# ConvGLU by block products: seven for eight, up-projection and down-projection in two phases

## The chip, the cores and the metric

The program runs on one core of a Trainium2 chip. TensorE (PE) multiplies, VectorE (DVE), ScalarE (ACT) and GpSimd (POOL) work on SBUF tiles of 128 partitions, DVE and ACT read PSUM as well, and SyncE (SP) issues most DMA transfers. Each engine works through its own queue in a fixed order. The metric is the device time of one execution in microseconds (us).

## The reference

Two transformer layers over 1024 tokens of width 1024; layer 0 carries 256 context tokens too. In each layer attention is followed by this tail (`FF` is 2816):

```python
def _conv_ffn(h, w_up, conv_w, conv_b, w_down):
    gate, val = jnp.split(h @ w_up, 2, axis=-1)          # each [tokens, 2816]
    gate = conv over 3 neighbouring tokens, per feature, + conv_b
    return (jax.nn.silu(gate) * val) @ w_down

x = _layer_norm(ALPHA * x + g1 * y, ln1)                 # y: attention @ w_out
h = x * (1 + sc2) + sh2
x = _layer_norm(ALPHA * x + g2 * _conv_ffn(h, ...), ln2)
```

## The kernel before, in words

Every product is made in float32r as three passes: both operands are split into a high and a low part (`split_hi` L408 on POOL or L404 on ACT, `split_lo` L412 on DVE or POOL), and `three` multiplies high by high, high by low and low by high. Activations lie feature-major: features on partitions, tokens on the free axis, in chunks of 512 tokens (two; in layer 0 a third of 256 context tokens).

`layer_tail(l)` projects the attention's output, applies LN1 (`ln1`, with L1321 making the scaled rows and L1343 the residual, kept in SBUF as `acc`), then runs the ConvGLU over 22 tiles `f` of 128 features, and LN2 in `after`. For each tile the loop calls `up(f, 0)`, the gate's product (48 matmuls for each chunk of 512 tokens: 8 blocks of 128 input features, 3 passes, 2 chunks), then `down(f - 1)`, then `conv(f)`, then `up(f, 1)`, the value's product, then `glu(f)`. `down(f - 1)` multiplies the finished tile with its 128 rows of `w_down`: 8 output tiles by 2 chunks by 3 passes, 48 matmuls, each triple into a PSUM bank of its own that DVE adds to `acc` (L1400). `conv` is an ACT pass (L1367), two DVE passes (L1369, L1373) and Silu on ACT (L1377); `glu` is a DVE product (L1381) and the split of the result (ACT L404, DVE L412). The last two tiles are multiplied together after the loop by `last_down`. In layer 0 DVE also works at column sums of the next layer's `w_ada` (L552, eight instructions in each of the first 16 tiles).

The order of each engine's queue is set when the program is built: a scheduler places the recorded operations, engine by engine, from the order of the code and the pools' buffers. Weights are split by POOL ahead of their use.

## Time and profile before

| | us |
|---|---|
| median of 3 runs | 3625.1 (3624.45 to 3625.25) |
| the profiled execution: its span, which is its own time as far as it is recorded | 3624.5 |
| layer 0: ConvGLU tiles | about 1010 to 1867 |
| layer 1: ConvGLU tiles | about 2874 to 3566 |
| busy PE / DVE / ACT / POOL | 3444.8 / 2252.0 / 1281.6 / 1668.7 |

The rows quoted further down give one instruction's mean duration (in ns), or a stretch of time in us. A matmul's busy time is longer than its pace, since matmuls overlap: the pace is read from a run of them in the chain of waits, not from the mean. "Idle before" is how long an engine stood still in front of the instructions of a group, and the name behind the arrow is what ended it; such idle time costs nothing by itself when PE is busy beside it.

### The profile page before, as it was taken

Reading aid. Unit: us, or ns where it says so; the run is one execution under the profiler, and the core shown is the slowest. Engines: PE = TensorE matmul, PEld = TensorE weight load, DVE = VectorE, ACT = ScalarE, POOL = GpSimd, SP = SyncE. Lnnn points to the kernel's source line nnn. Section 1 sums busy time; section 2 is a strip of 40 time slices with the busy share of each in tenths; the row PEclk is TensorE's granted clock in tenths of the full one; section 3 lists DMA queues with packets and bytes.
Section 4 is the critical chain, followed back from the end, with each engine's and each line's share of the span. In section 5 each row is a group of like instructions: output and inputs, shape, how many; then the busy total and the mean of one; then the engine's idle time right before and its main releaser. Section 6 shows DMA issues by size and latency. Waiting matters only on the chain.

```text
span 3624.5 us, 50952 instructions
## 1 busy us (share of the span) xinstructions
PE 3444.8 (95%) x19450; PEld 2949.6 (81%) x19450; DVE 2252.0 (62%) x3434; ACT 1281.6 (35%) x2393; POOL 1668.7 (46%) x1804
## 2 busy tenths in 40 slices
PE   7998899979899999999998999999999999999997
PEld 5987787877788888888886787999997788888885
DVE  6687787873666666655455544777774555445555
ACT  4222777762411111111025334777773301111002
POOL 4532787643422222232223523888886533333333
PEclk9999999999999999999999999999999999999998
DMA  6367411664333322211104267233323211111111
GB/s 211 111 203 217 108 46 48 166 181 139 117 108 96 93 88 82 82 53 41 36 19 125 82 242 231 57 79 76 80 66 114 85 47 47 53 47 47 53 35 47
DMA packets 311952, 349.52 MB, mean 96 GB/s; under 512 B 19157, under 2 KB 233597, under 8 KB 311709
## 3 DMA queue, kind: packets, MB, share of 16 engines
q1 hardware_dynamic: 298508, 319.66, 30.4%
q10 hardware_dynamic: 11424, 18.94, 1.4%
q0 software_dynamic: 1776, 7.67, 0.6%
q8 instruction: 153, 2.51, 0.3%
q14 instruction: 91, 0.74, 0.1%
HBM read 275.04 MB, written 71.11 MB: 96 GB/s over the span
## 4 chain that ended last, share of the span: by engine, by line
PE 74%; POOL 8%; DVE 8%; issue 5%; DMA 4%; ACT 2%; SPq 0%; ACTq 0%; POOLq 0%; DVEq 0%
PE pu L417 29%; PE pd L417 15%; PE psum L194 7%; PE psum L335 5%; PE pso L417 4%; PE psum L304 4%; POOL p L264 3%; PE psq L417 2%; PE ps_f L417 2%; PE ps_tu L417 1%; DVE aa L552 1%; PE pw L417 1%; POOL pl L312 1%; DMA bias<-in_l_rpb_dram 1%; POOL st L261 1%
## 5 line engine op out<-in xcount | busy, mean ns | idle before, releaser
L1400 DVE SCALAR_TENSOR_TENSOR acc<-pd,mods,acc 128x512 f32<-128x512 f32 (+1 forms) x800 | 525.0, 697 | 267.0 <-PE pd L417 252.3
L408 POOL TENSOR_SCALAR fh_u<-fr_u 128x1024 fp32r<-128x1024 f32 x88 | 95.0, 1079 | 857.6 <-PE pu L417 479.9
L417 PE MATMUL pd<-ah,fh_d 128*128 128x512 f32 (+1 forms) x880 | 331.7, 377 | 6.3 <-DVE acc L1400 3.8
L417 PE MATMUL pd<-al,fh_d 128*128 128x512 f32 (+1 forms) x880 | 326.0, 370 | 0.5 <-DVE al L412 0.5
L417 PE MATMUL pd<-ah,fl_d 128*128 128x512 f32 (+1 forms) x880 | 325.9, 370 | 0.0
L194 PE MATMUL psum<-k,q 96*128 96x512 f32 (+1 forms) x1152 | 272.3, 373 | 6.7 <-DMA k<-kr_scr 4.0
L417 PE MATMUL pu<-h_1l,fh_u 128*128 128x512 f32 x704 | 275.1, 391 | 2.1 <-POOL h_1l L412 2.1
L417 PE MATMUL pu<-h_0h,fh_u 128*128 128x512 f32 x704 | 275.3, 391 | 0.0
L417 PE MATMUL pu<-h_0h,fl_u 128*128 128x512 f32 x704 | 275.0, 391 | 0.0
L417 PE MATMUL pu<-h_0l,fh_u 128*128 128x512 f32 x704 | 274.9, 391 | 0.0
L417 PE MATMUL pu<-h_1h,fh_u 128*128 128x512 f32 x704 | 274.3, 390 | 0.0
L417 PE MATMUL pu<-h_1h,fl_u 128*128 128x512 f32 x704 | 274.0, 389 | 0.0
L1381 DVE TENSOR_TENSOR cv<-cv,pu 128x1280 f32<-128x1280 f32 (+1 forms) x44 | 59.6, 1355 | 295.7 <-PE pu L417 289.1
L194 PEld LDWEIGHTS psum<-k,q 96*128 96x128 f32 x1152 | 196.4, 192 | 35.3 <-issue 4.4
L412 POOL TENSOR_TENSOR fl_u<-fr_u,fh_u 128x1024 fp32r<-128x1024 f32 x88 | 212.4, 2413 | 7.3
L552 DVE SCALAR_TENSOR_TENSOR aa<-aw,silu_late,aa 128x512 f32<-128x512 f32 x224 | 190.5, 880 | 37.1 <-DMA aw<-in_l_w_ada_dram 34.9
L417 PEld LDWEIGHTS pd<-ah,fh_d 128*128 128x128 f32 x880 | 166.1, 189 | 58.2 <-DVE acc L1400 5.1
L1377 ACT ACTIVATE cv<-cv 128x1280 f32<-128x1280 f32 (+1 forms) x44 | 51.4, 1169 | 443.0 <-DVE cv L1373 443.0
L264 POOL TENSOR_SCALAR p_m<-p_m,st_m 128x640 f32<-128x640 f32 x256 | 201.8, 801 | 12.6
L1367 ACT ACTIVATE cv<-pu,vec 128x1280 f32<-128x1280 f32 (+1 forms) x44 | 58.2, 1322 | 417.5 <-PE pu L417 417.5
L320 DVE TENSOR_TENSOR pl_m<-psum,ph_m 128x512 fp32r<-128x512 f32 x256 | 175.0, 684 | 37.7 <-ACT ph_m L314 36.7
L304 PE MATMUL psum<-ident,p_m 128*128 128x128 f32 x1280 | 192.9, 273 | 2.5 <-DVE pl_m L320 2.2
(499 smaller groups left out, 9817.1 us busy)
## 6 DMA issues: line engine op xcount, KB each, us to landing
aw<-in_l_w_ada_dram SPq DMA_DIRECT2D x96, 512.0 KB
fr_u<-in_l_w_up_dram SPq DMA_DIRECT2D x88, 512.0 KB
fr_d<-in_l_w_down_dram SPq DMA_DIRECT2D x44, 512.0 KB
fr_o<-in_l_w_out_dram SPq DMA_DIRECT2D x30, 512.0 KB
v<-v_scr SPq DMA_DIRECT2D x17, 640.0 KB
k_b<-k_scr SPq DMA_DIRECT2D x16, 640.0 KB
v_scr<-vev SPq DMA_DIRECT2D x40, 256.0 KB
k<-k_scr SPq DMA_DIRECT2D x15, 640.0 KB
```

Source lines behind the costliest of these rows:

```text
L194: nc.tensor.matmul(u["s"][bank][:, c:e], q[:, qc], ks, start=pi == 0, stop=pi == len(u["passes"]) - 1)
L264: nc.gpsimd.tensor_scalar(pt, pt, st[:, j, 7:8], 0.0, op0=ALU.mult, op1=ALU.add)
L304: nc.tensor.transpose(tp[:, off + bi * P : off + bi * P + P], pts[j][:, c : c + P], ident)
L320: nc.vector.tensor_tensor(pl[:, :w], tps[g][:, :w], ph[:, :w].bitcast(F32), ALU.subtract)
L335: nc.tensor.matmul(u["av"][:, q0 : q0 + bw], u["v"][:, kt, :], m[:, off : off + bw], start=first and part == 0, stop=last and part == 1, s ...
L408: nc.gpsimd.tensor_scalar(dst, src, 1.0, 0.0, op0=ALU.mult, op1=ALU.add)
L412: e.tensor_tensor(dst, src, hi.bitcast(F32), ALU.subtract)
L417: nc.tensor.matmul(ps, s, m, start=i == 0, stop=i == n - 1)
L552: nc.vector.scalar_tensor_tensor(accs[c], w, sck, accs[c], op0=ALU.mult, op1=ALU.add)
L1367: nc.scalar.activation(cv, g[:, :nt], AF.Identity, bias=vec(l, "cb", f), scale=vec(l, "w1", f))
L1381: nc.vector.tensor_tensor(cv, cv, v[:, :nt], ALU.mult)
L1400: nc.vector.scalar_tensor_tensor(acc[m][ci], ps[:, :cn], mod(l, ci // 2, 5, m), acc[m][ci], op0=ALU.mult, op1=ALU.add)
```

## The change

Gate and value are now one product of a 2 by 2 block matrix: rows are the two halves of the 1024 input features, columns are gate and value (weights A11, A12 for the gate, A21, A22 for the value, with 512 input features each), and the other operand's blocks are the halves of features by the two chunks of tokens. Seven block products replace eight. Each is 12 matmuls of 512 columns, so a tile takes 84 for 96. The weights' four sums (`weight_sums`: L1201, L1204, L1207, L1211) are made for every tile, the tokens' four sums (`token_sums`) once per layer in `ln1(1)`; every operand is split as before, the weights now by ACT (high) and POOL (low; the first product's by DVE in layer 1, the value's first half by DVE in layer 0). The context's chunk in layer 0 is still multiplied plainly.

The loop over tiles no longer calls `down`. After every second tile `keep_pair` makes the four sums of the activated pair and stores seven operands in DRAM (`a_scr`); the context's activations go to `ac_scr`, the last two tiles' to `al_scr`, and the residual of LN1 goes to `res_scr`. After the loop the pools are closed, and a second phase runs over the pairs, two at a time (five groups): for each of the seven products it splits weights and stored operands and makes 4 row tiles of 6 matmuls for each pair. P2, P3 and P4 are added to `acc` at once, the others collect in SBUF tiles `Q` and are added at the end. The last two tiles are multiplied plainly as before.

```diff
-        def up(f, part, order):
-            wh, wl = load_w(
-                cols(A[f"l{l}_w_up"][:, part * FF + f * P : part * FF + (f + 1) * P]), f"u{l}_{f}_{part}"
-            )
...
+    def weight_sums(A11, A12, A21, A22, tmp, eng):
+        e = [nc.vector if x == "dve" else nc.gpsimd for x in eng]
+        S1, S2 = tmp("s1"), tmp("s2")
+        e[0].tensor_tensor(S1, A21, A22, ALU.add)
+        yield "A21", A21
+        yield "P1", A11
+        e[1].tensor_tensor(S2, S1, A11, ALU.subtract)
+        yield "P6", S2
+        yield "P5", S1
+        e[2].tensor_tensor(A21, A11, A21, ALU.subtract)
+        yield "P7", A21
+        yield "P2", A12
+        yield "P4", A22
+        e[3].tensor_tensor(S2, A12, S2, ALU.subtract)
+        yield "P3", S2
+    def token_sums(B11, B12, B21, B22, tmp, eng):
+        e = [nc.vector if x == "dve" else nc.gpsimd for x in eng]
+        T1, T2, T3, T4 = (tmp(f"t{i}") for i in range(1, 5))
+        e[0].tensor_tensor(T1, B12, B11, ALU.subtract)
+        e[1].tensor_tensor(T2, B22, T1, ALU.subtract)
+        e[2].tensor_tensor(T3, B22, B12, ALU.subtract)
+        e[3].tensor_tensor(T4, B21, T2, ALU.subtract)
+        return {"P5": T1, "P6": T2, "P7": T3, "P4": T4}
...
+                xs = tl("ax", (512,), f"rs{l}_{ci}_{m}")[:, :cn]
+                nc.scalar.activation(xs, pb, AF.Identity, bias=der[:, 1, m : m + 1], scale=der[:, 0, m : m + 1])
+                nc.sync.dma_start(res_scr[l][m * P : (m + 1) * P, c0 : c0 + cn], xs)
...
+                for m, h in rows:
+                    whole[8 + m] = h
+                    if m < 4:
+                        continue
+                    parts(operand["P3"], m - 4, h, "dve")
+                    q = whole.pop(m - 4), whole.pop(m + 4), whole.pop(m), whole.pop(m + 8)
+                    sums = token_sums(
+                        *q, lambda n: tl("b", (512,), f"h{l}_{n}_{m}"), ("dve", "dve", "pool", "dve")
+                    )
+                    for i, p in enumerate(("P6", "P5", "P7", "P4")):
+                        parts(operand[p], m - 4, sums[p], "pool" if i % 2 else "dve")
...
+            b = [ps1(f"pu{l}_{f}_{i}") for i in range(3)]
+            bank = {"P1": b[0], "P2": b[0], "P6": b[1], "P7": b[1], "P4": b[1], "P5": b[2], "P3": b[2]}
+            for what, src in weight_sums(
+                *raw, lambda s: tl("b", (4, P), f"{s}_{l}_{f}"), ("dve", "pool", "dve", "dve")
+            ):
+                if what == "A21" and l:
+                    continue
+                w = tl("st", (2, 4, P), f"w{what}_{l}_{f}", F32R)
+                split_hi(w[:, 0], src, "act")
+                split_lo(w[:, 1], src, w[:, 0], "dve" if n == 0 else "pool")
...
+                mm_product(bank[what], w, operand[what], what in ("P1", "P6", "P5"))
+                if what == "P1":
+                    nc.scalar.copy(p1, b[0])
+                elif what == "P6":
+                    nc.vector.tensor_tensor(g[:, hi], b[1], p1, ALU.add)
...
+                elif what == "P3":
+                    nc.vector.tensor_tensor(g[:, hi], b[2], g[:, hi], ALU.add)
...
-            if prev is not None and not end:
-                down(f - 1, prev, range(len(chunks)))
+            g, v, px = up(f)
+            cv = conv(f, g, "c4", NX, "")
+            nc.vector.tensor_tensor(cv, cv, v, ALU.mult)
...
+            if f >= NF - 2:
+                nc.sync.dma_start(al_scr[l][f - NF + 2], cv)
+            elif f % 2:
+                keep_pair(f // 2, before, cv)
...
+                        nc.sync.dma_start(r, w_down[f * P : (f + 1) * P, i * 512 : i * 512 + 512])
...
+                nc.sync.dma_start(r, a_scr[l][j, i])
...
+            for ci in range(len(chunks)):
+                residual_in(ci)
+            for first in range(0, NF // 2 - 1, 2):
+                js = (first, first + 1)
...
+                    xs = [tokens(j, what) for j in js]
+                    for r in range(4):
+                        ps = bank(f"pd{l}_{first}_{what}_{r}")
+                        mm_rows(ps, r, ws, xs, 512)
...
+            for r in range(4):
+                q1, q6, q5, q7 = (Q[p][r] for p in ("P1", "P6", "P5", "P7"))
+                gated(0, r, q1)
...
+                nc.vector.tensor_tensor(q5, q5, q7, ALU.add)
+                gated(1, 4 + r, q5)
```

Two places of the queues are wanted later. The first is DVE in layer 1 around the convolution of tile 7 (`cv1_7` is tile 7 of layer 1, `pd1_6` the down-projection of tile 6, `wP1_1_8` and `ur1_8` weights of tile 8). Before:

```order
L1400 SCALAR_TENSOR_TENSOR acc1_1_7_27392<-pd1_6_1_7_29779,mods_1_86,acc1_1_7_27392 128x512
L1369 SCALAR_TENSOR_TENSOR cv1_7_29784<-pu1_7_0_29655,vec_1_79,cv1_7_29784 128x1023
L1373 SCALAR_TENSOR_TENSOR cv1_7_29784<-pu1_7_0_29655,vec_1_79,cv1_7_29784 128x1023
L1381 TENSOR_TENSOR cv1_7_29784<-cv1_7_29784,pu1_7_1_29795 128x1024
L412 TENSOR_TENSOR al1_7_29846<-cv1_7_29784,ah1_7_29845 128x1024
L1400 SCALAR_TENSOR_TENSOR acc1_0_0_27377<-pd1_7_0_0_29910,mods_1_86,acc1_0_0_27377 128x512
```

With the change, from the last combination of tile 7's gate to the first of tile 8's:

```order
L1491 TENSOR_TENSOR g1_7_30620<-pu1_7_2_30619,g1_7_30620 128x512
L1497 SCALAR_TENSOR_TENSOR cv1_7_30741<-g1_7_30620,vec_1_79,cv1_7_30741 128x1023
L412 TENSOR_TENSOR wP1_1_8_30779<-ur1_8_00_30762,wP1_1_8_30779 128x512
L1500 SCALAR_TENSOR_TENSOR cv1_7_30741<-g1_7_30620,vec_1_79,cv1_7_30741 128x1023
L1532 TENSOR_TENSOR cv1_7_30741<-cv1_7_30741,v1_7_30621 128x1024
L1219 TENSOR_TENSOR a1_t2_3_30748<-cv1_7_30741,a1_t1_3_30747 128x512
L1221 TENSOR_TENSOR a1_t4_3_30750<-cv1_7_30741,a1_t2_3_30748 128x512
L1201 TENSOR_TENSOR s1_1_8_30776<-ur1_8_10_30766,ur1_8_11_30768 128x512
L1207 TENSOR_TENSOR ur1_8_10_30766<-ur1_8_00_30762,ur1_8_10_30766 128x512
L1211 TENSOR_TENSOR s2_1_8_30777<-ur1_8_01_30764,s2_1_8_30777 128x512
L1478 TENSOR_TENSOR g1_8_30773<-pu1_8_1_30771,p1_1_8_30775 128x512
```

Before, tile 7's convolution is followed by the evictions of its own down-projection, and no weight of tile 8 is DVE's. Now the low part of tile 8's first weight stands between the two passes of tile 7's convolution, and tile 8's sums `s1` and A21' stand behind tile 7's product and the sums `t2` and `t4` of the pair.

The second is ACT at the same place, before (`ah` is the high part of an activated tile):

```order
L404 CAST ah1_6_29639<-cv1_6_29578 128x1024
L1367 ACTIVATE cv1_7_29784<-pu1_7_0_29655,vec_1_79 128x1024
L1377 ACTIVATE cv1_7_29784<-cv1_7_29784 128x1024
L404 CAST ah1_7_29845<-cv1_7_29784 128x1024
L1367 ACTIVATE cv1_8_29990<-pu1_8_0_29861,vec_1_79 128x1024
L1377 ACTIVATE cv1_8_29990<-cv1_8_29990 128x1024
```

and with the change (`p1` is a copy of product P1 out of PSUM):

```order
L1483 COPY g1_7_30620<-pu1_7_0_30617 128x512
L1496 ACTIVATE cv1_7_30741<-g1_7_30620,vec_1_79 128x1024
L404 CAST wP1_1_8_30779<-ur1_8_00_30762 128x512
L1503 ACTIVATE cv1_7_30741<-cv1_7_30741 128x1024
L1476 COPY p1_1_8_30775<-pu1_8_0_30770 128x512
L404 CAST wP6_1_8_30796<-s2_1_8_30777 128x512
```

Six of the seven high parts of tile 8's weights now stand behind the copy of its own first product, and so behind tile 7's Silu. POOL at that place, with the change (`s2` is A21 + A22 - A11):

```order
L1220 TENSOR_TENSOR a1_t3_3_30749<-cv1_7_30741,cv1_6_30603 128x512
L1204 TENSOR_TENSOR s2_1_8_30777<-s1_1_8_30776,ur1_8_00_30762 128x512
L412 TENSOR_TENSOR wP6_1_8_30796<-s2_1_8_30777,wP6_1_8_30796 128x512
L412 TENSOR_TENSOR wP5_1_8_30812<-s1_1_8_30776,wP5_1_8_30812 128x512
L412 TENSOR_TENSOR wP7_1_8_30828<-ur1_8_10_30766,wP7_1_8_30828 128x512
```

Tile 8's `s2`, and with it every low part but the first, stands behind `t3`, which reads tile 7's finished product. On SP, at the end of the loop, the store of tile 21 (`al_scr`, L1538) is followed by 16 loads of the residual (L1619, 128x512 f32 each), eight of `w_down` (L1583, 128x512) with, in layer 1, two of the last LayerNorm's vectors (128x1024) among them, and only then by the first stored operands (L1600); in layer 0 by 24 residual loads, eight of them 128x256, and four of the context's activations.

## Rows read from the trace of the kernel before

**Rows 1.** The page, busy time of the engines over the span.

```profile
PE 3444.8 (95%) x19450; PEld 2949.6 (81%) x19450; DVE 2252.0 (62%) x3434; ACT 1281.6 (35%) x2393; POOL 1668.7 (46%) x1804
```

**Rows 2.** The page, the chain that ended last, by engine and line.

```profile
PE 74%; POOL 8%; DVE 8%; issue 5%; DMA 4%; ACT 2%; SPq 0%; ACTq 0%; POOLq 0%; DVEq 0%
PE pu L417 29%; PE pd L417 15%; PE psum L194 7%; PE psum L335 5%; PE pso L417 4%; PE psum L304 4%; POOL p L264 3%; PE psq L417 2%; PE ps_f L417 2%; PE ps_tu L417 1%; DVE aa L552 1%; PE pw L417 1%; POOL pl L312 1%; DMA bias<-in_l_rpb_dram 1%; POOL st L261 1%
```

**Rows 3.** The chain of waits in layer 1 around tile 4: start us, us, what.

```profile
2880.89 21.62 PE pu L417 x94
2902.51 10.88 PE pd L417 x48
```

**Rows 4.** The page, groups: busy us, mean ns of one | idle before, releaser.

```profile
L417 PE MATMUL pu<-h_1l,fh_u 128*128 128x512 f32 x704 | 275.1, 391 | 2.1 <-POOL h_1l L412 2.1
...
L1377 ACT ACTIVATE cv<-cv 128x1280 f32<-128x1280 f32 (+1 forms) x44 | 51.4, 1169 | 443.0 <-DVE cv L1373 443.0
...
L1367 ACT ACTIVATE cv<-pu,vec 128x1280 f32<-128x1280 f32 (+1 forms) x44 | 58.2, 1322 | 417.5 <-PE pu L417 417.5
```

**Rows 5.** Groups of DVE by form, same columns, whole run.

```profile
L1400 DVE SCALAR_TENSOR_TENSOR acc<-pd,mods,acc 128x512 f32<-128x512 f32 x640 | 447.8, 750 | 248.5 <-PE pd L417 248.4
...
L320 DVE TENSOR_TENSOR pl_m<-psum,ph_m 128x512 fp32r<-128x512 f32 x256 | 175.0, 684 | 37.7 <-ACT ph_m L314 36.7
...
L1369 DVE SCALAR_TENSOR_TENSOR cv<-pu,vec,cv 128x1023 f32<-128x1023 f32 x44 | 56.1, 1275 | 23.8 <-ACT cv L1367 23.8
...
L1381 DVE TENSOR_TENSOR cv<-cv,pu 128x1024 f32<-128x1024 f32 x22 | 26.9, 1222 | 164.8 <-PE pu L417 164.8
...
L552 DVE SCALAR_TENSOR_TENSOR aa<-aw,silu_late,aa 128x512 f32<-128x512 f32 x224 | 190.5, 880 | 37.1 <-DMA aw<-in_l_w_ada_dram 34.9
...
L412 DVE TENSOR_TENSOR al<-cv,ah 128x1024 fp32r<-128x1024 f32 x22 | 43.4, 1975 | 24.5 <-ACT ah L404 24.5
...
L412 DVE TENSOR_TENSOR h_1l<-tmpa,h_1h 128x512 fp32r<-128x512 f32 x8 | 6.0, 744 | 1.2 <-ACT h_1h L404 1.2
...
L412 DVE TENSOR_TENSOR hr<-ht,hh 128x512 fp32r<-128x512 f32 x8 | 10.3, 1294 | 2.0 <-POOL hh L408 1.9
...
L1321 DVE TENSOR_SCALAR tmpa<-pba,der 128x512 f32<-128x512 f32 x31 | 24.4, 807 | 15.4 <-PE pba L1319 5.6 <-POOL h_0l L412 5.0 <-POOL h_1l L412 4.0
```

**Rows 6.** Groups of ACT by form, same columns, whole run.

```profile
L310 ACT COPY pr_m<-psum 128x512 f32<-128x512 f32 x64 | 37.5, 586 | 23.2 <-PE psum L304 23.2
...
L1377 ACT ACTIVATE cv<-cv 128x1024 f32<-128x1024 f32 x22 | 23.3, 1060 | 263.1 <-DVE cv L1373 263.1
...
L404 ACT CAST wh_in<-wr_in 128x512 fp32r<-128x512 f32 x36 | 21.7, 619 | 27.2 <-DVE aa L550 13.0 <-DVE evf L948 4.6 <-DMA arow<-ar 4.5
```

**Rows 7.** Groups of POOL by form, same columns, whole run.

```profile
L312 POOL TENSOR_TENSOR pl_m<-pr_m,ph_m 128x512 fp32r<-128x512 f32 x64 | 82.3, 1285 | 5.4
...
L412 POOL TENSOR_TENSOR aal<-aa,aah 128x512 fp32r<-128x512 f32 x32 | 46.3, 1457 | 41.6 <-ACT aah L404 41.6
```

**Rows 8.** Timeline of DVE and ACT, layer 1: start us, us, instruction.

```profile
3013.33 1.28 DVE L1373 SCALAR_TENSOR_TENSOR cv<-pu,vec,cv 128x1023 f32<-128x1023 f32 x1
3014.70 1.06 ACT L1377 ACTIVATE cv<-cv 128x1024 f32<-128x1024 f32 x1 [13.02 <-DVE cv L1373]
```

**Rows 9.** Timeline of PE at the longest wait of layer 0's first tiles.

```profile
1006.55 0.28 PE L417 MATMUL pu<-h_2h,fl_u 128*128 128x256 f32 x1
1010.67 0.80 PE L417 MATMUL pd<-ah,fh_d 128*128 128x512 f32 x1 [3.85 <-DVE acc L1400]
1011.27 0.63 PE L417 MATMUL pd<-al,fh_d 128*128 128x512 f32 x1
1011.70 0.63 PE L417 MATMUL pd<-ah,fl_d 128*128 128x512 f32 x1
```

**Rows 10.** Windows: us, then per engine busy (instructions), granted clock, DMA share, GB/s.

```profile
1010.00:1030.00 20.00, 19.32 (x87) 16.52 (x88) 17.05 (x25) 1.28 (x1) 0.00 (x0) 0.85 0.25 80
...
2140.00:2200.00 60.00, 57.78 (x304) 49.56 (x303) 25.54 (x45) 18.86 (x40) 9.89 (x14) 1.00 0.69 254
```

More of the change, by code (lines that the diff above doesn't have):

```diff
@@ new lines, in token_sums @@
+    def token_sums(B11, B12, B21, B22, tmp, eng):
[6 more added lines that the diff above has]
+        return {"P5": T1, "P6": T2, "P7": T3, "P4": T4}
+    res_scr = [dram.tile([D, NT], F32, name=f"res_scr{l}") for l in range(2)]
@@ L1170, in layer_tail @@
+    a_scr = [dram.tile([NF // 2 - 1, 7, P, 512], F32, name=f"a_scr{l}") for l in range(2)]
+    al_scr = [dram.tile([2, P, NX], F32, name=f"al_scr{l}") for l in range(2)]
+    ac_scr = dram.tile([NF, P, NCTX], F32, name="ac_scr")
+    PRODUCTS = ("P1", "P2", "P3", "P4", "P5", "P6", "P7")
     def layer_tail(l, after, kept=None):
@@ L1213, in layer_tail @@
-        if l == 0:
-            place("aw")
-        acc = [[feature_tile(ci, f"acc{l}_{ci}_{m}") for ci in range(len(chunks))] for m in range(KB)]
+        es_h, es_1 = ExitStack(), ExitStack()
+        H = kept[0] if kept else es_h.enter_context(wait_pool("hop0", "right"))
+        th = pool_tiles(H, {"b": 40 if l == 0 else 32})
+        T = es_1.enter_context(wait_pool(f"tail{l}", "left"))
+        pp = es_1.enter_context(wait_pool(f"psT{l}", space=PSUM))
+        four = {"fw": "c4", "fr": "c4", "aw": "c4", "c5": "c4", "aa": "b", "ax": "b", "xr": "b", "st": "c4"}
@@ L1312, in back, with normaliser, normalise @@
-        def back(ci, zs, name, scales, dst, residual):
-            c0, cn = chunks[ci]
-            hh, hl = dst
-            for m in range(KB):
+        def normaliser(acc, pool, tl, ps1):
+            def normalise(ci, j, name, residual=None, tag="c5", later=None):
+                z = tl(tag, (D,), f"z{name}_{ci}_{j}")
+                for half in range(2):
+                    pt = ps1(f"pt{name}_{ci}_{j}_{half}")
+                    for m in range(4):
+                        nc.tensor.transpose(
+                            pt[:, m * P : (m + 1) * P], acc[ci][:, 4 * half + m, j * P : (j + 1) * P], ident
+                        )
+                    zh = z[:, half * 512 : half * 512 + 512]
+                    if residual is None:
+                        nc.scalar.copy(zh, pt)
+                    else:
+                        nc.vector.scalar_tensor_tensor(
+                            zh, residual[:, half * 512 : half * 512 + 512], ALPHA, pt, op0=ALU.mult, op1=ALU.add
+                        )
+                with tc.high_priority(offset=50):
+                    mv, rs = ln_stats(z, pool, f"{name}_{ci}_{j}")
+                if later is not None:
+                    later.append((mv, rs))
+                elif j % 2:
+                    nc.vector.tensor_scalar(rs[:, 1:2], mv[:, 0:1], rs[:, 0:1], -1.0, op0=ALU.mult, op1=ALU.mult)
+                    nc.scalar.activation(z, z, AF.Identity, bias=rs[:, 1:2], scale=rs[:, 0:1])
+                else:
+                    nc.vector.tensor_scalar(z, z, mv[:, 0:1], rs[:, 0:1], op0=ALU.subtract, op1=ALU.mult)
+                return z
+            return normalise
@@ L1317, in back, with back_rows @@
+        def back_rows(ci, zs, name, scales, residual, tl, ps1, order=range(KB)):
+            cn = chunks[ci][1]
+            for m in order:
                 pb = ps1(f"pb{name}_{ci}_{m}")
@@ L1459, in layer_tail @@
                 ada_finish(1, ps1("ps_af1"))
-        K = {"l": l, "T": T, "tl": tl, "ps3": ps3, "ps1": ps1, "acc": acc, "chunks": chunks,
-             "chunk_tiles": chunk_tiles, "feature_tile": feature_tile, "normalise": normalise, "back": back,
-             "load_w": load_w, "last_down": lambda ci, which=slice(0, 2), **kw: last_down(left[which], ci, **kw)}
+        es_1.close()
+        es_h.close()
+        if kept:
+            kept[2].close()
+        es_t = ExitStack()
+        T = es_t.enter_context(wait_pool(f"down{l}", "left"))
@@ new lines, in back @@
+        def back(ci, zs, name, scales, dst, residual):
+            for m, h in back_rows(ci, zs, name, scales, residual, tl, ps1):
+                parts(dst, m, h, "pool" if m % 2 else "dve")
+        K = {"l": l, "T": T, "tl": tl, "ps3": ps3, "ps1": ps1, "chunks": chunks,
+             "chunk_tiles": lambda kind, ci: block_tiles(tl, f"{kind}{l}_{ci}", chunks[ci][1]),
+             "feature_tile": feature_tile, "normalise": normaliser(acc, T, tl, ps1), "back": back,
+             "load_w": load_w, "last_down": last_down}
@@ L1760, in tile_hybrid_block @@
     py = keep.enter_context(wait_pool("y1", "right"))
-    y1 = [
-        tuple(py.tile([P, KB, 512], F32R, name=f"y1_{ci}{s}", tag="a16", bufs=4) for s in "hl") for ci in range(2)
-    ]
+    y1 = [block_tiles(pool_tiles(py, {"b": 32}), f"y1_{ci}", 512) for ci in range(2)]
     with ExitStack() as es:
```

446 lines of the change are left out of this document (292 added, 154 removed).

## The prediction

> **What bounds the kernel now.** I read the page's busy times first, then the chain that ended last, then the chain of waits of one ConvGLU tile, then the groups of DVE, ACT and POOL by form. The reader is to see four things. TensorE is busy for 95% of the span, the other engines for 62, 35 and 46% [rows 1]. The up-projection `pu` alone is 29% of the chain and the down-projection `pd` 15% [rows 2]. In layer 1 the chain runs through these two without a wait: 96 matmuls of `pu` and 48 of `pd` per tile. Their pace is 10.88 us / 48 = 226.7 ns [rows 3], not the 391 ns that the group of `pu` shows as the mean of one [rows 4]: instructions overlap, and only the pace counts for the sum. And the convolution between the two products waits freely: Silu's instructions have 443.0 us idle in front of them, the pass before it 417.5 [rows 4], at no cost, because the previous tile's down-projection and weights split a tile ahead keep PE fed meanwhile.
>
> **What goes.** A tile has 84 matmuls for 96, so 12 x 226.7 ns = 2.72 us; 44 tiles give 119.7. In the down phase 168 matmuls do what 4 x 48 = 192 did: 24 x 226.7 = 5.44 us a group, ten groups, 54.4. Together 174 us, were PE still the only bound. DVE loses 640 evictions of 0.750 us [rows 5]; they lay beside PE, so nothing for them.
>
> **What comes, layer 1's tiles.** Before, a tile's convolution had a down-projection and the value's product to hide under. Now all seven products come first, and the next tile's weights are prepared by the same three queues behind the convolution. From P3's last matmul of tile 7 to P6 of tile 8 the queues force this chain (DVE, ACT and POOL pieces shown with the change): DVE's combination out of PSUM (0.69, as `pl_m` with 0.684 [rows 5]); ACT's Identity pass (1.06, by Silu of the same size [rows 6]); DVE pass 1.28; DVE low part of P1's weight (0.75, by `h_1l` 0.744); DVE pass 1.28; Silu 1.06; DVE product 1.22; t2 0.75; t4 0.75; s1 0.75 [rows 5]; POOL s2 1.35, between 1.285 and 1.457 [rows 7]; ACT high part 0.62 [rows 6]; POOL low part 1.35. That is 12.9. A handoff between engines costs about 0.06 (DVE's pass of 3013.33 ends at 14.61, Silu starts at 14.70 [rows 8]); with eleven of them 13.6. P1 of tile 8 (2.72 us) runs inside. P6's third matmul waits for the low part, and 70 matmuls of 226.7 ns = 15.9 us follow, so the tile takes 29.5 us. From an even to an odd tile `t2`, `t4` and the sums are out of the way: 0.69 + 1.06 + 1.28 + 0.75 + handoffs = 4.2 until P1's third matmul, 2.3 for the rest of P1; its copy out of PSUM stands behind Silu and takes 0.59; high part 0.62, low part 1.35, so P6's third matmul at about 9.3, and the tile takes 25.1. The mean is 27.3 against 21.76 for the up part before: +5.5 x 22 = **+122 us**, the 2.72 already taken off. Bounds: at the cheapest rows, without handoffs, +100; with the five SBUF-to-SBUF steps of DVE at the 1.294 us of `hr` [rows 5], +160.
>
> **Layer 0's tiles.** The same chain, lengthened: ACT makes two high parts (1.24) for P1, POOL its low part, and steps of 0.88 (L552 [rows 5]) stand among the sums. Odd to even: the product ends at 7.0; A21's low part, t2, t4, the first aa step and s1 bring DVE to 10.9, POOL works off P1's low part, t3 and `aal` (1.457 [rows 7]) until 11.2; PE waits for `aal`, runs P1 until 14.0; copy, high part, low part: 16.7. Even to odd: P1's third matmul at 8.45, P6's at 13.6. Plus 15.9, the context's matmuls apart: 32.6 and 29.4, against 21.76. The last six tiles have no column sums and take 29.4 both ways. 16 x 9.3 + 6 x 7.7 = **+195 us**; bounds +150 (L552 out of the way) and +240 (slow subtractions).
>
> **The clock.** After PE's wait of 3.85 us in layer 0 the next three matmuls stand 0.60, 0.43 and 0.42 us apart [rows 9], about twice 226.7 ns: the 1.2 GHz level. The window after it was granted 0.85 of 20 us: 3.0 us lost [rows 10]. With the change every tile has a wait of 4 us or more ahead of P1 and another ahead of P6. Part of the slower time lies inside the chain (P1 of an odd-to-even step). I take 2 us a tile, 44 x 2 = **+88**, between 0 and 132. The Trainium skill says the same of loops in "TensorE: Matmul & The Clock Gate", section "HAM oscillation — how this bites in real kernels": bursts of matmuls with a wait between them start cold each time, so the transition is paid once per burst instead of once per kernel. The trace before agrees at the single places where PE waits; by the rule the term would be its full 132, by a warm chip 0.
>
> **The change of phase.** SP's store of tile 21 waits for that tile's product, 7 us after the last matmul. Behind it stand 16 residual loads of 256 KB, eight of weights, two of vectors of 512 KB and the first two operands: 16 x 0.262 + 8 x 0.262 + 2 x 0.524 + 2 x 0.262 = 7.9 MB, in layer 0 by the same count 8.4. The densest window moves 254 GB/s [rows 10]: 31 to 33 us. With splits about 42 us without a matmul, where the trace before has none. The first group's operands also land slower than PE uses them: +6. Against 27.2 saved by the layer's five groups that is +21 a layer, **+42**; bounds 0 (loads overlap more than the queue says) and +74 (two thirds of that rate, 16 us more a layer). Later groups have weights 3 products ahead: 38.1 us of PE against some 32 of POOL and 32 to 40 of DVE, taken as hidden.
>
> **The ends.** In `ln1(1)` DVE now does 2 x 0.807 (L1321), one low part, three sums and two more low parts for each of four rows: 6.1 us for 2.4, +15 a layer, since P6 needs all rows: **+30** (0 to 40). After the last product DVE still has six passes of 0.75 and a 1024 wide low part of 1.975 [rows 5] before `last_down` can go on: 6.5 a layer, **+13** (0 to 25).
>
> The sum is made against the profiled span, 3624.5, which lies 0.6 under the median: 122 + 195 + 88 + 42 + 30 + 13 = +490, so **4115 us**.
>
> **A second page.** The Trainium skill's "GPSIMD Engine Reference", section "Specifications", has GpSimd share its SBUF interfaces with VectorE, with contention where a DVE instruction has two SBUF inputs. The trace shows the spread that this would give: 0.744 for one kind of 512 wide subtraction, 1.294 for another [rows 5]. By the rule DVE's sums beside POOL's low parts would go to the upper bounds above.
>
> **Rivals.** (1) PE stays the bound: the preparation of a tile's weights gets far enough ahead of the convolution that only phase changes and ends remain: 3624.5 - 174 + 96 (42 idle and 6 at the first group, a layer) + 43 (the ends) = about 3590. It decides where the waits a tile come to under (3625 - 3590) / 44 = 0.8 us. For it: POOL and ACT are busy for under half of the span [rows 1], so there is room. Against it: the queues are fixed, and s1 stands behind t4, s2 behind t3, six high parts behind Silu. Chance 0.07. (2) No change: the waits come to some 0.8 us a tile and pay back just what the matmuls save; the same rows speak against it. 3625, 0.03. (3) The same mechanism, but milder: no cost of clock, column sums that fit into waits, overlapping loads; 3624.5 + 100 + 150 + 0 to 42 + 0 to 43, so 3875 to 3960, and down to 3720 where steps of the chain overlap that I count one behind the other. 0.13. (4) Worse: the upper bounds together (the slow subtractions everywhere, 132 for the clock, a phase change at two thirds of the rate): 4115 + 38 + 45 + 44 + 32, about 4275, in any case above 4240. For it: DVE and POOL both work between SBUF and SBUF in these stretches, which before they mostly did not. 0.09. (5) That the change does not do what it says: 12 matmuls a product and 168 a group stand in the queue, so I give this nothing.
>
> **The numbers.** The forecast as worked out, 3960 to 4240, has 0.68. The range 3850 to 4280 takes in its whole stretch, half of (3) and half of (4). Faster by over 0.2% (7 us, about what a measurement of this kernel can tell from no change) 0.07, within 0.2% 0.03, slower 0.90.
>
> **What would show it.** PE's busy share falls to about 80%, and its idle time in the tiles ends on ACT (high parts, P1) and POOL (low parts of P6), some 10 us from odd to even tiles and 6 from even to odd; tiles of layer 1 alternate between about 30 and 25 us plus the clock's share; the granted clock is below 1 throughout both stretches; each change of phase shows about 40 us of PE idle with DMA over 200 GB/s. The prediction is wrong if PE's waits in the tiles are under 2 us, if the odd and even tiles do not differ, or if the clock holds at full speed.

## The result: 1.191 times as long, and the profile after

The changed kernel takes 4316.75 us (median; 4312.71 to 4317.41) beside 3624.77 for the kernel before: a ratio of 1.1908, 95% interval 1.1891 to 1.1925. It is slower, as forecast, but by 692 us where +490 was predicted, 37 us beyond the range.

First the page of the kernel after: busy times, the granted clock in 40 slices, and the costliest groups of the up products, with ACT's copy ahead of the convolution.

```profile
PE 3539.4 (82%) x18682; PEld 2929.4 (68%) x18682; DVE 2514.5 (58%) x3600; ACT 1679.4 (39%) x3199; POOL 2141.6 (50%) x2182
...
PEclk8999999987887888879997999999998888889798
...
L1422 PE MATMUL pu<-h_P6h,wP 128*128 128x512 f32 x352 | 174.2, 566 | 176.4 <-ACT wP L404 151.4
L1422 PE MATMUL pu<-h_P1h,wP 128*128 128x512 f32 x352 | 184.9, 598 | 142.7 <-ACT wP L404 123.6
...
L1483 ACT COPY g<-pu 128x512 f32<-128x512 f32 x44 | 25.9, 588 | 480.1 <-PE pu L1422 480.1
```

PE falls from 95% [rows 1] to 82%. The idle time in front of `pu` was 2.1 us in the group of [rows 4]; now 319 us stand ahead of P6's and P1's matmuls, and what ends most of it is ACT's cast of a weight (L404). No other engine is above 58%: no engine's own work fills the span. Whether the order of the queues does it is tried below. The same instruction is slower too: 566 and 598 ns a matmul where [rows 4] had 391, at a granted clock of 7 or 8 tenths in most slices of the tiles (of the 40 of `PEclk`, those from the 10th to the 18th and from the 31st to the 37th).

The span divided into stages, of the kernel after and then of the kernel before, whose stretches of tiles begin at the first down product (us, then busy us of PE, PEld, DVE, ACT, POOL, granted clock, DMA share, GB/s). After: layer 0's tiles up to 15, the last six, the change of phase, the down phase, the last tiles with the head of layer 1; then layer 1's tiles, change of phase and down phase.

```profile
1019.10:1713.40 694.30, 510.60 (x2264) 400.60 (x2264) 366.54 (x401) 160.75 (x264) 235.88 (x158) 0.83 0.30 99
1713.40:1897.60 184.20, 150.90 (x662) 119.31 (x661) 75.09 (x86) 44.15 (x71) 58.45 (x42) 0.85 0.14 47
1897.60:1932.60 35.00, 0.00 (x0) 0.00 (x0) 9.55 (x20) 6.57 (x12) 2.27 (x2) 0.55 0.79 276
1932.60:2208.20 275.60, 259.91 (x1320) 218.47 (x1320) 186.76 (x254) 97.39 (x181) 189.16 (x135) 0.96 0.35 110
2208.20:2630.60 422.40, 356.66 (x1700) 286.49 (x1699) 202.30 (x327) 148.34 (x270) 135.46 (x144) 0.89 0.40 133
3314.00:3987.60 673.60, 519.15 (x1836) 377.76 (x1836) 269.13 (x287) 156.60 (x238) 230.47 (x163) 0.87 0.19 60
3987.60:4019.30 31.70, 0.00 (x0) 0.00 (x0) 5.89 (x7) 4.19 (x6) 4.28 (x4) 0.54 0.77 279
4019.30:4241.00 221.70, 203.48 (x840) 160.51 (x840) 152.72 (x183) 85.45 (x155) 190.19 (x132) 0.96 0.40 126
```

```profile
1010.70:1867.00 856.30, 856.30 (x4417) 722.03 (x4418) 507.94 (x724) 97.69 (x92) 226.43 (x133) 1.00 0.24 71
1867.00:2227.40 360.40, 332.88 (x1698) 270.47 (x1696) 195.96 (x311) 149.44 (x271) 134.86 (x143) 0.99 0.45 149
2902.40:3566.20 663.80, 663.80 (x2930) 549.67 (x2929) 335.67 (x402) 68.78 (x62) 204.77 (x118) 1.00 0.15 45
```

Before, PE has no idle time in the two stretches of tiles, at full clock; after, 217 us in layer 0's (694.3 + 184.2 less 510.6 and 150.9) and 154 in layer 1's, at 0.83 to 0.87. In layer 0 a good part of it, 88 us, stands ahead of the two matmuls of the column sums (`ps_a`); their rows among PE's waits of that stretch (us in total, times, longest):

```profile
PE ps_a L417 <- ACT aah L404: 59.6, 8, 7.5
PE ps_a L417 <- POOL aal L412: 28.8, 8, 3.6
```

The columns below set the growth of each stage of the span against the terms of the prediction:

| stage (both layers) | predicted | measured |
| --- | --- | --- |
| tiles (122 + 195 + clock 88) | +405 | +466 (layer 0: 269, layer 1: 198) |
| change of phase and down phase | +42 | +72 (35.8 a layer) |
| `ln1(1)` up to the first tile's products | +30 | +71 (34 and 37) |
| ends, with the head of layer 1 | +13 | +77 (62 and 16) |
| elsewhere | 0 | +4 |

Two borders in the kernel before are set by count, since products of two kinds alternate there: the tiles of layer 1 as 22 of 21.62 us ahead of 3566.2 (the first products run among the last rows of `ln1(1)`), and the down products of layer 0 as about 275 us (272 at the pace of their matmuls, 283 from start to start). The split between these rows is good to about 10 us; their sum doesn't depend on it.

**The chain in a tile.** The timeline of the kernel after, layer 1, from tile 7 to tile 8 (start us, us, engine, line, instruction, in brackets what it waited for):

```profile
3675.32 0.69 DVE L1491 TENSOR_TENSOR g<-pu,g 128x512 f32<-128x512 f32 x1 [2.03 <-PE pu L1422]
3676.10 1.24 ACT L1496 ACTIVATE cv<-g,vec 128x1024 f32<-128x1024 f32 x1 [5.41 <-DVE g L1491]
...
3677.90 0.50 PE L1422 MATMUL pu<-h_P1h,wP 128*128 128x512 f32 x1 [2.62 <-ACT wP L404]
...
3679.18 1.28 DVE L1500 SCALAR_TENSOR_TENSOR cv<-g,vec,cv 128x1023 f32<-128x1023 f32 x1
...
3680.55 1.06 ACT L1503 ACTIVATE cv<-cv 128x1024 f32<-128x1024 f32 x1 [2.70 <-DVE cv L1500]
...
3681.64 1.23 DVE L1532 TENSOR_TENSOR cv<-cv,v 128x1024 f32<-128x1024 f32 x1 [1.18 <-ACT cv L1503]
...
3682.90 0.69 DVE L1219 TENSOR_TENSOR a_t<-cv,a_t 128x512 f32<-128x512 f32 x1
3682.95 1.77 POOL L1220 TENSOR_TENSOR a_t<-cv,cv 128x512 f32<-128x512 f32 x1 [18.57 <-DVE cv L1532]
...
3683.63 1.63 DVE L1221 TENSOR_TENSOR a_t<-cv,a_t 128x512 f32<-128x512 f32 x1
...
3685.19 0.68 DVE L1201 TENSOR_TENSOR s<-ur,ur 128x512 f32<-128x512 f32 x1
...
3685.95 1.77 POOL L1204 TENSOR_TENSOR s<-s,ur 128x512 f32<-128x512 f32 x1 [1.23 <-DVE s L1201]
...
3687.74 1.14 ACT L404 CAST wP<-s 128x512 fp32r<-128x512 f32 x2 [3.66 <-POOL s L1204]
...
3688.41 0.79 PE L1422 MATMUL pu<-h_P6h,wP 128*128 128x512 f32 x1 [4.96 <-ACT wP L404]
```

This is the forecast chain, step for step: the gate's combination (L1491), ACT's pass, DVE's two passes (L1500 is the second), Silu, the product, `t2` (L1219), `t4` (L1221), `s1`, `s2`, the high part. PE waits 2.62 us ahead of P1 and 4.96 ahead of P6. Longer than priced are ACT's Identity pass (1.24 for 1.06), `t4` (1.63 for 0.75) and `s2` (1.77 for 1.35); DVE's other subtractions are a little shorter (0.68 and 0.69 for 0.75). From P3's last matmul to P6's third it takes 14.9 us on the mean of ten odd-to-even steps (13.6 predicted) and 11.0 from even to odd (9.3), the first such step left out; the rest is 19.0 and 17.5 (15.9 and the clock), so a step takes 33.8 and 28.5 us.

### The profile page after: what moved, and what is told of

It is laid out like the page before. It is cut to its first block, busy times and chain, and to the rows that moved or that the text cites. A ratio compares the mean times of both kernels' runs of the same rounds, so it can differ in the third digit from the quotient of the medians.

```text
span 4314.9 us, 52712 instructions
## 1 busy us (share of the span) xinstructions
PE 3539.4 (82%) x18682; PEld 2929.4 (68%) x18682; DVE 2514.5 (58%) x3600; ACT 1679.4 (39%) x3199; POOL 2141.6 (50%) x2182
## 5 line engine op out<-in xcount | busy, mean ns | idle before, releaser
L1612 PE MATMUL pd_P<-aP,dP 128*128 128x512 f32 x1680 | 407.5, 401 | 100.6 <-ACT aP L404 78.3
L1612 PEld LDWEIGHTS pd_P<-aP,dP 128*128 128x128 f32 x1680 | 320.8, 193 | 184.3 <-ACT aP L404 82.6
L412 POOL TENSOR_TENSOR wP<-ur,wP 128x512 fp32r<-128x512 f32 x154 | 222.7, 1469 | 356.0 <-ACT wP L404 356.0
L412 POOL TENSOR_TENSOR wP<-s,wP 128x512 fp32r<-128x512 f32 x132 | 176.2, 1349 | 295.0 <-ACT wP L404 291.3
L1422 PE MATMUL pu<-h_P6h,wP 128*128 128x512 f32 x352 | 174.2, 566 | 176.4 <-ACT wP L404 151.4
L1422 PE MATMUL pu<-h_P1h,wP 128*128 128x512 f32 x352 | 184.9, 598 | 142.7 <-ACT wP L404 123.6
L251 ACT ACTIVATE p_m<-psum,st_m 128x1024 f32<-128x1024 f32 (+2 forms) x192 | 187.0, 984 | 14.2 <-DVE st_m L244 13.3
L314 ACT CAST ph_m<-psum 128x512 fp32r<-128x512 f32 x256 | 151.0, 591 | 87.4 <-PE psum L304 41.5
L335 PE MATMUL psum<-ph_m,v 128*128 128x256 f32 x640 | 175.4, 301 | 1.0 <-DVE y_m L353 1.0
L335 PE MATMUL psum<-pl_m,v 128*128 128x256 f32 x640 | 164.3, 282 | 0.0
```

The source lines that it names most:

```text
L251: nc.scalar.activation(pt, src if bias is None else pt, AF.Exp, bias=st[:, j, 2:3], scale=1.0 if bias is None else -1.0, accum_out=st[:, j ...
L314: nc.scalar.copy(ph[:, :w], tp[:, :w])
L335: nc.tensor.matmul(u["av"][:, q0 : q0 + bw], u["v"][:, kt, :], m[:, off : off + bw], start=first and part == 0, stop=last and part == 1, s ...
L412: e.tensor_tensor(dst, src, hi.bitcast(F32), ALU.subtract)
L1422: nc.tensor.matmul(ps, st, mv, start=start and i == 0, stop=i == len(pairs) - 1, skip_group_check=True)
L1612: nc.tensor.matmul(ps, st, mv, start=start and i == 0, stop=i == len(pairs) - 1, skip_group_check=True)
```

## The experiments

Theory 1 says that the tiles' time is the order of the three queues, which puts the next tile's weights behind the convolution. Its rivals: the loads and buffers, which would hold the weights back whatever the order; and the clock, at which PE takes nearly twice as long behind the waits. Each ratio is against the kernel before, measured beside it (3621.78 to 3622.64 us); gains are against the 4316.75 of the change. The 95% intervals reach 6 to 9 us to either side, so a gain of under 10 us is not clear of noise.

**The order, in part (e1).** The first four weights of layer 0's next tile and three of layer 1's, with their loads and sums, are issued ahead of the convolution:

```diff
-            g, v, px = up(f)
+            g, v, px = up(f, ahead)
+            ahead = start(f + 1) if f + 1 < NF else None
             cv = conv(f, g, "c4", NX, "")
```

> The changed kernel, with the next tile's loads, sums and its first splits (P1, P6, P5; in layer 0 A21 too) written ahead of the convolution of the tile before. Theory 1 (the waits in the tiles come from the order of the queues: weights of the next tile behind the convolution): PE's idle time in the tiles, 217 us in layer 0 and 154 in layer 1, falls to some 40 in all, and with it most of the 167 us that the lower clock costs there: 4317 - 330 - 140, about 3850 us. Rival (the engines simply have too much to do per tile, or the wait moves to P7, whose low part then stands behind the pair's t3): under 150 us gained, 4170 or more.

Measured: 3990.93 us, ratio 1.1015 (1.0995 to 1.1035), 326 us gained; clock 0.927 for 0.899. The expected 3850 us was not reached. From odd to even in layer 1 a step is 22.8 us for 33.8, but from even to odd still 25.3: high parts of P4's and P7's weights stand behind Silu as before, and PE waits up to 4.1 us for them. Layer 0's odd-to-even steps fall from 43.2 to 38.0 only, since the two matmuls of the column sums still wait for `aah` and `aal`, and P1 starts behind them, 11.5 us after P3's last matmul. So the order carries most, and how much was not settled by a partial move.

**The order, whole (e6).** From e1 on: all seven of the next tile's weights in layer 1 and six of eight in layer 0 ahead of the convolution, and the rows of layer 0's column sums too:

```diff
-    AHEAD = (4, 3)
+    AHEAD = (6, 7)
...
+            if rows is not None:
+                run(rows)
+                rows = None
             ahead = start(f + 1) if f + 1 < NF else None
             cv = conv(f, g, "c4", NX, "")
```

> As e1_ahead, with all the next tile's weights of layer 1 and six of eight of layer 0 split ahead of the convolution, and in layer 0 the sums over partitions of the tile before written ahead of it too. Theory 1 (order of the queues): what was left of the waits (70 us in layer 1, behind P7's and P4's high parts on ACT; 111 in layer 0, ahead of the sums' two matmuls) goes, with its lower clock of 62 us: 3991 - 200, about 3790 us. Rival (POOL's or DVE's own work per tile is the bound now): 3900 or more.

Measured: 3836.87 us (1.0593; 1.0576 to 1.0611), 480 us gained, 47 less than expected. PE's waits in layer 1 from 3080 to 3500 us (us in total, times, longest), and the window itself:

```profile
PE pu L1424 <- DVE g L1489: 12.4, 11, 1.1
```

```profile
3080.00:3500.00 420.00, 407.82 (x1786) 334.54 (x1787) 278.65 (x285) 154.13 (x231) 251.60 (x157) 1.00 0.29 95
```

In 420 us only 12 are idle, none of them for a weight, and the clock is 1.00 again. A step is 19.04 us from even to odd, 84 x 226.7 ns to the hundredth, and 20.47 from odd to even. Instructions, buffers and bytes are those of the change; only their order differs. The loads move ahead with the rest, but in the change itself none of ACT's casts behind the first tile waits for one; DVE's `s1` of layer 1 does ten times, for at most 1.1 us, and one low part of POOL's in layer 0 for 3.7. Theory 1 is shown for layer 1. In layer 0 it holds for the larger part: steps are 32.1 and 28.0 us for 43.2 and 40.4, and of the 621 us from 1030 to 1651 PE still waits 56, 35 of them for DVE's `g`; what holds DVE back there was not tried.

**The clock (e2, e2b).** Filler matmuls of no use to the output, between the waits, keep PE busy, at the price of one of the eight PSUM buffers; e2 has them in both layers, e2b (its edit is shown) in layer 1 alone, sized to the waits there:

```diff
                 if what == "P1":
+                    keep_warm(f"b{l}_{f}", w, operand["P1"], (4 if f % 2 else 26) if l else 0)
+                elif what == "P3" and f + 1 < NF:
+                    keep_warm(f"a{l}_{f}", w, operand["P3"], 12 if l else 0)
```

> The changed kernel with matmuls that nobody reads put into PE's waits, ahead of P1 and of P6 of each tile (9 to 24 of 512 columns, fewer than the wait is long), so that PE stands still for little while the chain of the other engines is as before. Theory 2 (the clock at 1.2 GHz after the waits costs 167 us in the tiles): most of it comes back, 4317 - 130, about 4190 us, with the granted clock in the tiles above 0.97. Rival (the clock's share lies inside the chain, and the chain alone sets the time): no change, 4300 to 4330.

Measured: 4301.46 us (1.1877; 1.1853 to 1.1901), 15 gained. It decides nothing: in layer 0 the fillers ran into the products (odd-to-even steps 46.2 us for 43.2) and took back what the clock gave.

> The changed kernel with matmuls that nobody reads in layer 1's tiles alone: 12 of 512 columns ahead of P1, and ahead of P6 26 in even tiles and 4 in odd ones, so that they fill the measured waits of 3.0, 5.5 and 1.6 us but for some 0.5 us. If the lower clock is what makes a tile of layer 1 longer than its chain says (33.8 and 28.5 us for 29.5 and 25.1), the tiles fall to about 31 and 26.5 us, 2.4 x 22 = 50 us: about 4265 us. If the chain of the other engines alone sets them, no change within 10 us.

Measured: 4286.0 us (1.183; 1.1812 to 1.1848), 31 gained. The granted clock is 1.00 through layer 1's tiles (0.87 in the change), and the steps fall to 32.1 and 27.0, 1.6 us on the mean: 36 us over 22 tiles, under the 50 expected. In the change the 512 wide matmuls of these tiles that follow the one before without a wait took some 73 us more than at 226.7 ns each; counted so, this run still has 19, mostly starts behind a wait, so some 54 belong to the lower level. Of the 18 that did not come back, 15 lie in P1 of the ten odd-to-even steps: it takes longer in the change, but P6's third matmul comes 14.9 us after P3 in both runs, so PE would have waited there anyway. Without the clock's share a step is still 29.6 us, above the 27.3 of the prediction's chain: the chain itself was priced too short.

**DVE beside POOL (e13).** The pair's `t3` goes from POOL to DVE:

```diff
-                ("dve", "dve", "pool", "dve"),
+                ("dve", "dve", "dve", "dve"),
```

> The changed kernel with the pair's sum t3 on DVE instead of POOL, so that it no longer runs beside t4. In the changed kernel's trace t4 takes 1.63 us beside t3 (1.77 on POOL), for 0.69 alone. If the two engines disturb each other there, t4 falls to 0.7 and the odd to even step of layer 1 to about 33.6 us (t3's 0.7 comes in, 0.95 goes, s2 starts sooner): total -5 to -15 us. If t4's length is its own, the step grows by t3's 0.7 us: +15 us.

Measured: 4287.26 us (1.1834; 1.1816 to 1.1852), 29.5 gained by giving DVE 20 instructions more, where 5 to 15 were expected. Groups by form of DVE and POOL, of the kernel after (`a_t` are `t1` to `t4` of a pair; L1218 is `t1`, L1219 `t2`, L1221 `t4`, L1211 the sum A12 - S2), then the row of `t4` in this run:

```profile
L1211 DVE TENSOR_TENSOR s<-ur,s 128x512 f32<-128x512 f32 x44 | 77.2, 1755 | 88.0 <-POOL wP L412 88.0
...
L1221 DVE TENSOR_TENSOR a_t<-cv,a_t 128x512 f32<-128x512 f32 x20 | 32.7, 1635 | 0.7
...
L1219 DVE TENSOR_TENSOR a_t<-cv,a_t 128x512 f32<-128x512 f32 x20 | 22.3, 1114 | 0.4
...
L1218 DVE TENSOR_TENSOR a_t<-cv 128x512 f32<-128x512 f32 x20 | 13.7, 687 | 0.3
...
L1204 POOL TENSOR_TENSOR s<-s,ur 128x512 f32<-128x512 f32 x44 | 76.5, 1738 | 36.8 <-DVE s L1201 36.1 <-POOL h_P4l L412 0.7
```

```profile
L1221 DVE TENSOR_TENSOR a_t<-cv,a_t 128x512 f32<-128x512 f32 x20 | 13.7, 682 | 0.0
```

The same subtraction takes 1635 ns while POOL works (on `t3` in layer 1, mostly on the low part `aal` in layer 0) and 682 when POOL does not; L1211, beside POOL's low parts, takes 1755. But not every DVE instruction beside POOL is slow: in the timeline above `t2` starts 0.05 us ahead of `t3` and takes 0.69 us, and `t3` takes 1.77. The one that starts second pays. So the mean of `t2`, 1114, is made of two: 1745 where POOL's `t3` started first (eight in layer 0) and 692 where `t2` did. `s2` is paid by POOL for the same reason: 1738 ns, where its subtractions of that size were 1285 in [rows 7].

**The change of phase (e3) and the head of layer 1 (e5, e7, e11).** e3 leaves out the loads of the residual ahead of the stored operands (ACT copies the first product of each accumulator instead, so DVE has 40 additions less); its edit is shown. e5 issues the first three loads of layer 1's `w_in` ahead of the last two tiles of layer 0:

```diff
-            for ci in range(len(chunks)):
-                residual_in(ci)
+            begun = set()
```

> The changed kernel without the residual's loads at the change of phase (the first product of each accumulator is copied in its place, so the residual of LN1 is left out of the result). If the change of phase is bound by the bytes in front of its first operands, the waits of 35.0 and 31.7 us fall by 5.2 and 4.2 MB at 277 GB/s, 19 and 15 us: 4317 - 34, about 4283 us. If it is bound by the chain behind them (tile 21, splits, first operands), under 10 us come back.

Measured: 4292.48 us (1.1848; 1.1824 to 1.1873), 24 gained. PE's wait for the first operands, layer 0, of the kernel after and then of e3 (us in total, times, longest):

```profile
PE pd_P L1612 <- ACT aP L404: 38.4, 3, 35.0
```

```profile
PE pd_P L1612 <- ACT aP L404: 27.4, 5, 21.6
```

The residual's loads are a good third of the wait (13.4 of 35.0 us; 10.2 of 31.7 in layer 1). Some 7 us are lost again in the phases behind, which take 3 us longer each.

> The changed kernel with the first three weight loads of the projections of layer 1 issued before the last two tiles of layer 0 are multiplied, instead of 54 us after the last product. If the head of layer 1 is slower than before (by some 60 us) because its first weights come late and the lower clock follows the waits, some 25 to 45 us come back: about 4280 us. If the head is slower for another reason (the order of LN2's steps), no change.

Measured: 4308.2 us (1.1893; 1.1872 to 1.1914), 8.6 gained, not clear of noise; the waits of the head for the high parts of `w_in` stay. e7 then gives the raw loads of the down phase buffers of their own (`fr` 3, `b` 39 for 45):

> The changed kernel with three SBUF buffers of their own for the weights as loaded in the second phase and the head of layer 1 (six fewer of the 45 half-size ones), as the kernel before has them. If the head of layer 1 loses its 62 us because its weight loads wait for matmuls of earlier weights in buffers of the same kind, the head comes back to within 20 us of before: 4317 - 40, about 4275 us. If it loses them by the order of LN2's steps, under 10 us come back; fewer half-size buffers could also cost the down phase up to 10 us a layer.

Measured: 4312.6 us (1.1905; 1.1887 to 1.1923), 4 gained, not clear of noise: the head's 62 us do not hang on the raw loads' buffers. e11 gives own buffers to the split weights of the down phase and the head (eight), and their raw loads (two; also one of LN2's tiles gets one of the eight):

```diff
-        slots = {"b": 45, "c4": 17, "acc512": 16, "acc256": 8}
+        slots = {"b": 45, "c4": 7, "fw": 8, "fr": 2, "acc512": 16, "acc256": 8}
...
-                    w = tl("c4", (2, 512), f"d{what}_{l}_{j}", F32R)
+                    w = tl("fw", (2, 512), f"d{what}_{l}_{j}", F32R)
```

> The changed kernel with the second phase's SBUF buffers divided as in the kernel before: eight of their own for split weights, two for weights as loaded, seven for the rest, for 17 in common; with that the casts of the first projection weights stand ahead of LN2's rows in ACT's queue again. If the head of layer 1 loses its 62 us because its split weights find no free buffer until late, about 40 us come back, 4275 us. If it is the order of PE's transposes or the lower clock from the stretch before, under 15 us.

Measured: 4286.79 us (1.1831; 1.1813 to 1.1849), 30 gained. The stretch of the head in this run:

```profile
2217.40:2599.00 381.60, 341.72 (x1700) 278.08 (x1699) 198.72 (x327) 150.74 (x271) 132.52 (x143) 0.94 0.45 150
```

422.4 us become 381.6 at the same count of matmuls; the down phases pay 9 and 3.5 back, having fewer buffers, and the waits ahead of them 1 and 2. So 40 of the head's 62 come from split weights that share their buffers with others, and from the order that follows: in ACT's queue the casts of `w_in`, which before stood ahead of the first chunk's LayerNorm rows, stood behind them in the change and stand ahead of them again in e11.

**What the fewer matmuls were worth at best (e9).** The kernel before, with one matmul in eight of both products left out and everything else as it was. A tile there has 96 matmuls of 512 columns in its up products (48 for the gate and 48 for the value, both chunks together), and 12 go; of the 48 of a down product 6 go (the second half of the edit, not shown):

```diff
-                    [p3 for k in range(KB) for p3 in three(wh[:, k, :], wl[:, k, :], hh[:, k, :], hl[:, k, :])],
+                    [p3 for k in range(KB - (ci < 2)) for p3 in three(wh[:, k, :], wl[:, k, :], hh[:, k, :], hl[:, k, :])],
...
```

> The kernel before, with as many matmuls of 512 columns left out as the change leaves out and nothing else: 12 of 96 in each tile's two up-products, 6 of 48 in each down-projection (so the products are incomplete). If a matmul left out is worth its pace of 226.7 ns while PE is the bound: 44 x 2.72 + 40 x 1.36 = 174 us, about 3450 us. If the convolution or the evictions (16 x 0.75 us in 9.5 us of matmuls) come to the front, less: 3500 or more.

Measured: 3507.18 us (0.9684; 0.9657 to 0.9711): 115 saved, not 174. PE's wait in layer 0's tiles of this run (us in total, times, longest):

```profile
PE pd L417 <- DVE acc L1401: 33.5, 13, 4.4
```

Layer 1 gives the full 87; in layer 0 DVE's evictions come to the front in the tiles that have column sums as well, and leave 30.

**Together (e8, e12).** e8 is e6 with e7, e12 is e6 with e11.

> e6_all_ahead and e7_own_tag together. The two touch different stretches, so their gains should add: e6_all_ahead's time less what e7_own_tag saves, about 3750 us by the two expectations; still over the 3622 us of the kernel before, since both changes of phase, ln1 and the ends are as they were.

Measured: 3831.93 us (1.0577; 1.0562 to 1.0593), 5 below e6, not clear of noise, and far from the 3750 expected, since neither e6 nor e7 gave what was expected of it.

> e6_all_ahead and e11_own_weights together: the sum of both gains, about 3800 us, if the head's loss is one of buffers; 3830 if not. In either case slower than the 3622 us of before: two changes of phase (some 80 us without matmuls), ln1 (55) and the layer 0 tiles' column sums stay.

Measured: 3812.51 us (1.0525; 1.0508 to 1.0543): the best version of the change, and still 190 us above the kernel before. Its tiles are those of e6; what remains is what neither edit touches, the changes of phase, `ln1(1)`, the ends and layer 0's steps (32.1 and 27.9 us, with the column sums in them).

## Why the prediction had the sign and the place, and missed the size

**The likeliest case held.** No order of the queues was found wrong: the chain stands in the timeline as written, odd and even steps differ (33.8 and 28.5), PE's share is 82% for "about 80%", and e6 takes 480 of the 692 us away by moving those instructions alone. Rival (1), PE stays the bound, needed waits under 0.8 us a tile; they are 7.6 ahead of P1 and P6 in the step shown. Rival (2) falls with it, and (3), the same mechanism at a lower price, by the time. Rival (4) is the one that came nearest in time, about 4275; of its parts the slow subtractions are shown (e13), the clock at its upper bound and the slow loads are not (e2b, and below).

**Where the 202 us are missing.** The ends are 64 us above their price, the tiles 61, `ln1(1)` 41, the changes of phase with the down phases 30.

**The step that failed: the ends.** It priced +13 for DVE's last passes and measured +77. The wait that it named is there (PE ahead of `last_down`, for L1622, 6.74 us), but the list of what the change touches ended at the ConvGLU: the head of layer 1 stood in the sum at nothing, without a reason given, and costs 62. It takes its weights from the same buffers as the down phase. SP's issues of `w_in` for layer 1, of the kernel before and then after (start us, us until the last of the group):

```profile
1836.34 61.40 SPq L1231 DMA_DIRECT2D fr_wi<-in_l_w_in_dram  x3
```

```profile
2262.17 29.20 SPq L1699 DMA_DIRECT2D fr_wi<-in_l_w_in_dram  x5
```

Before, the first stands 31 us ahead of the end of layer 0's tiles (1867); after, 54 us behind the end of its down phase (2208.2). e11 gives 40 of the 62 us back by buffers of its own and the order that follows from them. The other 22 are not settled; by e5 and e7 neither the early issue of three loads nor the raw buffers are worth more than some 15 us.

**Terms that were sized too small.** The tiles' +405 are +466. The clock's 2 us a tile were near, 1.6 in layer 1 (e2b); no run shows its price in layer 0. What was short is the chain: `t4` and `s2` by 0.9 and 0.4 us beside POOL, ACT's pass by 0.2; and two waits that no step named, PE for DVE's `g` and `v` out of PSUM ahead of P7 and P4, 0.3 and 0.4 us a tile each in layer 1:

```profile
PE pu L1422 <- ACT wP L404: 147.0, 43, 28.5
...
PE pu L1422 <- DVE v L1480: 9.3, 22, 0.4
...
PE pu L1422 <- DVE g L1478: 7.1, 19, 0.4
```

The first row holds the wait of 28.5 ahead of the layer's first tile, which is the term of `ln1(1)`: +71 for +30. DVE is busy for 31.1 of 34.4 us there in layer 0 and 29.5 of 31.5 in layer 1, so it is DVE's time, as the step had it. But a row takes 7.2 us where 6.1 was worked out, with subtractions beside POOL at 1648 ns (L1219 `h_t`); and the step took off the 2.4 us of a row before, which had cost nothing, because PE had the first tile's products to run beside those rows. The stretch from the first product on in layer 1, before and then after (columns as in the stages above):

```profile
2863.20:2902.40 39.20, 37.96 (x179) 29.94 (x178) 19.97 (x32) 17.95 (x25) 15.52 (x13) 1.00 0.13 41
```

```profile
3282.50:3314.00 31.50, 3.04 (x13) 2.20 (x13) 29.47 (x32) 17.51 (x30) 20.55 (x14) 0.63 0.18 67
```

So there was nothing to take off, which is 19 of the 41 us. In layer 1 another 15 lie ahead of these rows: the stretch up to the first product takes 121.6 us for 106.5, and PE waits 7.3 us in it for the statistics of LN1 where it waited 0.2. None of this was tried on its own.

In layer 0 P6's third matmul comes 3.3 us later than worked out (20.1 and 16.9 us). From odd to even P1 starts at 12.4 for 11.2, and its twelve matmuls then take 5.1 us for 2.7, 0.43 apart, with P1's copy and P6's parts behind them: here the clock's price is on the chain. e13 brings that third matmul 2.1 and 0.7 us forward and shortens the steps by 0.6 and 0.95; no run shows the clock's part. A handoff, by the way, was read as 0.06 us where the row quoted gives 0.09; over eleven that is 0.3.

**The change of phase.** The wait was sized too long, 35.0 and 31.7 us for 42: the loads ran at 276 and 279 GB/s where the densest window before had 254 [rows 10]. The phases behind it were sized too short: 275.6 us where the down products before took about 275, so that none of the 27.2 saved by the layer's five groups (168 matmuls each, for two pairs) arrives; in layer 1, where the count is exact, 221.7 for 217.6. PE is idle for 16 and 18 us in them, at a clock of 0.96: groups that were taken as hidden are not.

**The two pages.** The Trainium skill's "GPSIMD Engine Reference", section "Specifications", has contention where a DVE instruction with two SBUF inputs runs beside GpSimd; e13's 1635 and 682 ns agree. But the upper bounds that made all of DVE's sums slow were not the better price for that: in layer 1's chain `t4` alone was, and `t2` and `s1` took 0.69 and 0.68 us. Its "TensorE: Matmul & The Clock Gate", section "HAM oscillation — how this bites in real kernels", has the price of a cold start paid in each burst: the rows agree that it is paid (0.43 us a matmul behind the waits), but the full 132 us that the prediction set beside it would be 66 for layer 1's 22 tiles, and the filler gave 36.

## What to carry to other kernels

Before the saved matmuls are counted, write the chain through the in-order queues from the last product of one tile to the first of the next: here 12 matmuls less a tile (2.7 us) came with steps 7 to 12 us longer in layer 1, and the same instructions ahead of the convolution gave 480 us back. Then ask what the stage behind takes its buffers from, what PE did beside the work that now stands alone, and price an elementwise step between SBUF and SBUF twice, alone and beside GpSimd, when both engines share a chain. And ask what the saving is worth in the old order: 115 us of 174 here, since the engine next in line was close.
